# Attention inside a hybrid block: TensorE's order fixed by hand, transposes two key blocks ahead and in turn with products, low parts against the values' high part alone

## The chip, the cores and the metric

One Trainium2 chip, one core. The metric is the device time of one execution in microseconds (us), as a median of several runs.

## The reference, cut to what matters

The kernel computes a whole block of a streaming encoder: a norm, forgetting attention beside a state space model, gates, an output projection, a second norm and a convolutional feed-forward part. The change touches the attention alone:

```python
D_MODEL, SEQ, N_META = 1024, 1024, 16        # 16 meta tokens stand ahead: 1040 positions
ATTN_HEADS, ATTN_HEAD_DIM = 8, 64

def block(args):                             # one block of queries, all heads
    qb, fqb, qp = args
    s = jnp.einsum('bqhd,bkhd->bhqk', qb, k) * scale
    s = s + fq[..., None] - fk               # F[t] - F[s], cumulated log of the forget gate
    mask = k_pos[None, :] <= qp[:, None]
    s = jnp.where(mask[None, None], s, -1e30)
    p = jax.nn.softmax(s, axis=-1)
    return jnp.einsum('bhqk,bkhd->bqhd', p, v)
```

Everything is float32.

## The kernel before

**Float32 by halves.** TensorE is fed fp32r operands. A float32 number is split into a high and a low part, and a product becomes several matmuls. A projection takes three for each 128 of depth: high by high (L170), low by high (L171), high by low (L172).

**Tiles.** The queries are nine tiles: tile 0 has the 16 meta positions, tiles 1 to 8 have 128 each. A query tile c sees `KS[c] = 16 + 128 c` keys. The eight heads go in four pairs. While a pair is attended, TensorE also computes the next pair's queries and keys (`project_qk`, 16 matmuls of depth 128 by three for each part of 384, 384 or 272 columns) and some chunks of the gates (`gate_chunk`, 342 columns each, L499 reads them). These matmuls are called fill here. They write `mm`.

**Scores** (`scores`, for one query tile). Two matmuls (L825, L826) for each bank of at most 512 keys write `sp`, of which there are two PSUM buffers. Tile 7 has two banks (456, 456 keys), tile 8 has three (352, 352, 336). VectorE adds the forget row `fb` to a bank and takes the running least value (L831, into `pt` and `mx`); the diagonal 128 x 128 is a reduction of its own, against a masked copy `fm` from GpSimd (L814). So tile 7's second bank takes two reductions (328 and 128 wide), tile 8's third also two (208 and 128). Then ScalarE's exponential (L836), VectorE's reciprocal (L837), and GpSimd's multiplication (L838).

**Products** (`pv`, for one unit). A unit is one head and a pair of query tiles, (1,2), (3,4), (5,6) or (7,8), or the meta tile alone. The probabilities are transposed by TensorE, 128 x 128 each, into `tp` (two PSUM buffers); ScalarE copies that into the high part `th` (L872), VectorE makes the low part `tl` (L137). One group has two key blocks, up to four transposes, L868. The 16 meta keys have their own transposes (L854) and their own `tm` (one buffer, L855 on ScalarE, then L137 on VectorE). The values lie in `vt` as 128 columns for a head: 64 of their high part, 64 of their low part. Both `th` and `tl` are multiplied with all 128 columns (L891), `tm` likewise (L880), and sum up in one PSUM bank `po` (one buffer). At a unit's end ScalarE copies the lower half (L895) and VectorE adds the upper half (L896) into `ob`, which goes to DRAM.

**Order.** The program issues the scores of unit u+1 ahead of the products of unit u, and within a unit the transposes of the next group ahead of the products of this one. `fill()` releases a share of the fill at each group. It ties only the first matmul of a share, to the fifth last mark; beyond that a list scheduler with its own estimates of time decides where TensorE's instructions stand. PE, DVE, ACT, POOL and SP each work through their rows in order. The program text of one query tile's banks:

```python
for b in range(nb):
    ps = s_ps()                              # two PSUM buffers
    PE.matmul(ps, Qs, Ks, start=True, stop=False)
    PE.matmul(ps, qz, kl, start=False, stop=True)
    ...                                      # VectorE's reductions of this bank
```

Of the kernel before, what the change touches and what calls it, by code (L numbers as in the profile page):

```python
# [25 lines left out]
H = 8  # L26
# [32 lines left out]
def block_kernel(ctx, tc, x, meta, xbt, x0t, g1t, w_q, w_k, w_v, w_f, w_u, w_g, b_f, w_ao, lam_d, bw_d, cw_d,  # L59
# [25 lines left out]
    def po_ps():  # L85
        return pp.tile([P, 512], F, tag="po", name="po", bufs=1)
# [49 lines left out]
    def split_lo(eng, out_, src, hi):  # L136
        return eng.tensor_tensor(out_, src, hi.bitcast(F), ALU.subtract)  # L137
# [39 lines left out]
    def run(gen):  # L177
        for _ in gen:
            pass
# [612 lines left out]
    st_a = ExitStack()  # L792
    qps.append(pool(st_k, "qkB", side="left"))
    ap = pool(st_a, "attn", side="left")
    tm = ap.tile([P, 256], R, name="tm")
    GP.memset(tm.bitcast(F), 0.0)
    KS = [META + P * c for c in range(len(TILES))]
    qzero = [[ap.tile([P, P], R, name=f"qz{e}{j}") for j in range(2)] for e in range(2)]
    for e in range(2):
        for z in qzero[e]:  # L800
            GP.memset(z[64 - 64 * e:P - 64 * e].bitcast(F), 0.0)

    def scores(t_, e, c, fb):
        t, n = TILES[c]
# [11 lines left out]
        pt = ap.tile([P, L], F, tag="pt", name="pt", bufs=4)  # L816
        mx = ap.tile([P, 4], F, tag="mx", name="mx", bufs=4)
        low = 3e38
        nb = -(-kc // 512)
        w = -(-kc // nb // 8) * 8  # L820
# [1 line left out]
        for b in range(nb):  # L822
            a0, a1 = b * w, min(kc, b * w + w)
            ps = s_ps()
            PE.matmul(ps[:m_, :a1 - a0], Qs[:, t:t + m_], Ks[:, a0:a1], start=True, stop=False)  # L825
            PE.matmul(ps[:m_, :a1 - a0], qz[:, :m_], t_["kl"][:, a0:a1], start=False, stop=True)  # L826
            for lo, hi, src in ((a0, min(a1, dg), fb), (max(a0, dg), a1, None)):
                if hi <= lo:
                    continue
                s_ = fb[:n, lo:hi] if src is not None else fm[:n, lo - dg:hi - dg]  # L830
                V.tensor_tensor_reduce(out=pt[:n, lo:hi], in0=ps[:n, lo - a0:hi - a0], in1=s_, scale=-0.125,  # L831
                                       scalar=low, op0=ALU.add, op1=ALU.min, accum_out=mx[:n, ns:ns + 1])
                low = mx[:n, ns:ns + 1]
                ns += 1
        nm = ap.tile([P, 2], F, tag="nm", name="nm", bufs=4)
        S.activation(pt[:n, :kc], pt[:n, :kc], AF.Exp, bias=low, scale=-1.0, accum_out=nm[:n, 0:1])  # L836
        V.reciprocal(nm[:n, 1:2], nm[:n, 0:1])  # L837
        GP.tensor_scalar(pt[:n, :kc], pt[:n, :kc], nm[:n, 1:2], 1.0, ALU.mult, ALU.mult)  # L838
        return pt

    def pv(h, cs, pts, ob):
        e = h % 2
        t, n = TILES[cs[0]]
        w = n * len(cs)
        po = po_ps()
        groups = [(j, j + 1) for j in range(1, cs[-1], 2)]

        def order(grp):
            return grp[::-1] if grp[-1] > cs[0] else grp

        def meta_keys():
            tp = t_ps()
            for ci, p_ in enumerate(pts):
                PE.transpose(tp[:META, ci * n:ci * n + n], p_[:n, :META], ident[:n, :n])  # L854
            S.copy(tm[:META, :w], tp[:META, :w])  # L855
            split_lo(V, tm[32:32 + META, :w], tp[:META, :w], tm[:META, :w])

        def turn(grp):
            tp = t_ps()
            z = 0  # L860
            for gi, kk in enumerate(order(grp)):
                for ci, p_ in enumerate(pts):
                    k0 = TILES[kk][0]
                    o = (gi * len(pts) + ci) * n
                    if kk > cs[ci]:
                        z = o + n
                        continue
                    PE.transpose(tp[:, o:o + n], p_[:n, k0:k0 + P], ident)  # L868
            tw = len(grp) * w
            th = ap.tile([P, 512], R, tag="th", name="th", bufs=2)  # L870
            tl = ap.tile([P, 512], R, tag="tl", name="tl", bufs=2)
            S.copy(th[:, z:tw], tp[:, z:tw])  # L872
            split_lo(V, tl[:, z:tw], tp[:, z:tw], th[:, z:tw])
            return th, tl

        meta_keys()
        nxt = turn(groups[0]) if groups else None
        if groups:
            fill()
        marks.append(PE.matmul(po[:, :w], vt[:, 0, h, :], tm[:, :w], start=True, stop=not groups,  # L880
                               skip_group_check=True))
        for g_, grp in enumerate(groups):
            th, tl = nxt
            if g_ + 1 < len(groups):
                nxt = turn(groups[g_ + 1])
            fill()
            for gi, kk in enumerate(order(grp)):
                last = kk == order(groups[-1])[-1]
                q0 = n if kk > cs[0] else 0
                for t_ in (th, tl):  # L890
                    mk = PE.matmul(po[:, q0:w], vt[:, kk, h, :], t_[:, gi * w + q0:gi * w + w], start=False,  # L891
                                   stop=last and t_ is tl, skip_group_check=True)
            marks.append(mk)
        o_ = ob[64 * e:64 * e + 64, :w]
        S.copy(o_, po[64:, :w])  # L895
        V.tensor_tensor(o_, po[:64, :w], o_, ALU.add)  # L896

    GA = [2, 1, 1, 3]
    SLACK = 5
    QKN = 2 * len(BLK) * 3 * KD  # L900
    GAN = len(QBLK) * 3 * KD
    HOOKS = 2 * sum(1 + (c + 1) // 2 for c in range(1, len(TILES), 2))
    stream = iter(())
    left = [0, 0]
    marks = []

    def fill():
        k = -(-left[0] // max(1, left[1]))
        left[1] -= 1
        anchor = marks[-SLACK] if len(marks) >= SLACK else None  # L910
        for _ in range(k):
            if left[0] > 0:
                left[0] -= 1
                mm = next(stream, None)
                if mm is not None and anchor is not None:
                    tc.add_manual_dep(mm.ins, anchor.ins.name, mybir.DependencyInfo(
                        mybir.DependencyClass.NoSync, mybir.DependencyReason.DATA), reason="spread")
                    anchor = None

    def chain_(*gens):  # L920
        for g_ in gens:
# [16 lines left out]
    done = 0  # L938
    for pr in range(H // 2):
        fbs = []  # L940
        for e in range(2):
            fb = ap.tile([P, L], F, tag="fb", name="fb", bufs=2)
            SY.dma_start(fb, f_d[2 * pr + e].partition_broadcast(P))
            fbs.append(fb)
        gens, cnt = [], 0
        last_pair = pr == H // 2 - 1
        if not last_pair:
            qk_next = qk_tiles(pr + 1)
            gens.append(project_qk(pr + 1, qk_next))
            cnt += QKN  # L950
        for i in range(done, done + GA[pr]):
            gens.append(gate_chunk(i, ap, True))
            cnt += GAN
        done += GA[pr]
        stream = chain_(*gens)
        left[:] = [cnt, HOOKS]
        if pr == 0:
            for _ in range(24):
                next(stream)
                left[0] -= 1  # L960
        obs = {}

        def second(cs, e, pts):
            if e == 0:
                obs[cs] = ap.tile([P, 256], F, tag="ob", name="ob", bufs=1)
            pv(2 * pr + e, cs, pts, obs[cs])
            if e == 1:
                t, w = TILES[cs[0]][0], sum(TILES[c][1] for c in cs)
                if last_pair:
                    oh, ol = okeep[pr]  # L970
                    S.copy(oh[:, t:t + w], obs[cs][:, :w])
                    split_lo(V, ol[:, t:t + w], obs[cs][:, :w], oh[:, t:t + w])
                else:
                    SY.dma_start(o_d[P * pr:P * pr + P, t:t + w], obs[cs][:, :w])

        if last_pair:
            spare = qk_tiles(pr + 1)
            okeep[pr] = (spare["q0"], spare["q1"])
            okeep[0] = (spare["k0"], spare["k1"])
            of = spare["kl"].bitcast(F)  # L980
            SY.dma_start(of, o_d[:P])
            S.copy(spare["k0"], of)
            split_lo(GP, spare["k1"], of, spare["k0"])

        prev = None
        for n_unit, (cs, e) in enumerate(units):
            if 0 < pr < 3 and n_unit and n_unit % 2 == 0:
                out_weight_sums(4 * (pr - 1) + n_unit // 2 - 1, marks[-1])
            pts = [scores(qk, e, c, fbs[e]) for c in cs]
            if prev:  # L990
                second(*prev)
            prev = (cs, e, pts)
        second(*prev)
        run(stream)
        if pr < H // 2 - 1:
            qk = qk_next
    st_a.close()
    st_v.close()
    if "o_d" in dbg:
# [1050 lines left out]
```

## Time and profile before

| what | value |
|---|---|
| median of 3 runs | 1444.09 us (1443.51 to 1444.99) |
| profiled execution | 1441.98 us, span 1440.2 us |
| granted TensorE clock | 0.998 |
| instructions | 26318 |
| busy share of the span | PE 98%, PEld 93%, DVE 74%, ACT 50%, POOL 52% |
| attention stage | 339.27 to 619.73 us of the span |

The attention stage is counted here from the first fill matmul (L170) behind the values' projection (its last matmul, L130, starts at 339.04) to the first L170 behind the last L891. PE is TensorE's matmuls, PEld its weight loads, DVE VectorE, ACT ScalarE, POOL GpSimd, SP the queue that issues most DMAs. A row of the trace's timeline has a start in us, a duration in us, the engine, the line, the operation, output and inputs, and in brackets how long the engine was idle ahead of it and what released it. "x4" stands for four instructions that follow one another, with the time from the first's start to the last's end. Matmuls overlap: what counts for the pace is the time from one start to the next, not the duration of one.

### The profile page before, as it was taken

The numbers are of one execution on the slowest core, as the hardware profiler recorded it, in microseconds if no ns is written. First come the engines' busy times: TensorE is split into PE (matmuls) and PEld (weight loads), VectorE is DVE, ScalarE is ACT, GpSimd is POOL, SyncE is SP. The second block draws the span as 40 slices with busy tenths as digits, with TensorE's granted clock in tenths as the row PEclk, the third lists the DMA queues.
The fourth block names the chain that finished last, engine by engine and source line by source line (L and its number), as shares of the span: only waits on it lengthen the run. The fifth ranks groups of instructions, "written<-read, shape, count | busy, mean of one in ns | idle before, by whom it ended". The sixth has DMA issues, their size and how long they took to land.

```text
span 1440.2 us, 26318 instructions
## 1 busy us (share of the span) xinstructions
PE 1416.7 (98%) x9615; PEld 1337.7 (93%) x9615; DVE 1069.7 (74%) x2067; ACT 722.6 (50%) x1422; POOL 754.3 (52%) x824
## 2 busy tenths in 40 slices
PE   8999999999999999999999999999999999999997
PEld 8999999987999999999879999999999999887886
DVE  7999788843757676647469987888876876788767
ACT  7647585423646565533646443444444445643443
POOL 1642248632455546415861335555555545797795
PEclk9999999999999999999999999999999999999999
DMA  8776644531156322167964146667753327864443
GB/s 303 173 180 162 159 108 147 155 96 30 38 152 145 122 68 68 44 233 250 257 153 140 59 134 174 169 167 188 190 141 110 96 77 260 322 208 141 115 94 117
DMA packets 92966, 214.04 MB, mean 149 GB/s; under 512 B 15090, under 2 KB 22898, under 8 KB 92452
## 3 DMA queue, kind: packets, MB, share of 16 engines
q1 hardware_dynamic: 74132, 168.15, 35.5%
q0 software_dynamic: 17696, 41.29, 15.1%
q10 hardware_dynamic: 1008, 2.91, 0.6%
q8 instruction: 76, 1.25, 0.4%
q14 instruction: 54, 0.44, 0.1%
HBM read 170.88 MB, written 71.71 MB: 168 GB/s over the span
## 4 chain that ended last, share of the span: by engine, by line
PE 94%; DMA 2%; ACT 1%; DVE 1%; issue 1%; POOL 0%; SPq 0%; POOLq 0%; DVEq 0%; ACTq 0%
PE mm L172 5%; PE mm L170 5%; PE mm L171 5%; PE sp L233 4%; PE sp L232 4%; PE sp L234 4%; PE mm L232 3%; PE mm L234 3%; PE tp L232 3%; PE mm L233 3%; PE tp L233 3%; PE tp L234 3%; PE po L891 3%; PE tp L868 2%; PE mm L1573 2%; PE mm L1572 2%
## 5 line engine op out<-in xcount | busy, mean ns | idle before, releaser
L170 PE MATMUL mm<-xhi,whi 128*128 128x342 f32 (+2 forms) x480 | 157.7, 329 | 0.9 <-DVE q L137 0.9
L171 PE MATMUL mm<-xlo,whi 128*128 128x342 f32 (+2 forms) x480 | 155.9, 325 | 0.0
L172 PE MATMUL mm<-xhi,wlo 128*128 128x342 f32 (+2 forms) x480 | 155.7, 325 | 0.0
L1193 POOL TENSOR_TENSOR ov<-ov,og 128x1024 f32<-128x1024 f32 x21 | 50.8, 2421 | 119.4 <-ACT og L1192 117.1
L137 DVE TENSOR_TENSOR sw<-sf,sw 128x512 fp32r<-128x512 f32 x72 | 71.3, 990 | 45.9 <-ACT sw L1184 45.8
L1184 ACT CAST sw<-sf 128x512 fp32r<-128x512 f32 x72 | 44.9, 623 | 109.5 <-POOL sf L1331 69.9
L170 PEld LDWEIGHTS mm<-xhi,whi 128*128 128x128 f32 x480 | 90.4, 188 | 2.5 <-issue 1.7
L172 PEld LDWEIGHTS mm<-xhi,wlo 128*128 128x128 f32 x480 | 90.3, 188 | 0.6 <-issue 0.2
L171 PEld LDWEIGHTS mm<-xlo,whi 128*128 128x128 f32 x480 | 90.5, 189 | 0.3
L1331 POOL TENSOR_TENSOR sf<-raw,sf 128x512 f32<-128x512 f32 x36 | 61.7, 1714 | 39.2 <-DVE sw L137 39.1
L234 PE MATMUL mm<-xhi,sw 128*128 128x258 f32 (+1 forms) x288 | 81.0, 281 | 0.0
L232 PE MATMUL mm<-xhi,sw 128*128 128x258 f32 (+1 forms) x288 | 80.8, 280 | 0.0
L233 PE MATMUL mm<-xlo,sw 128*128 128x258 f32 (+1 forms) x288 | 80.7, 280 | 0.0
L1331 POOL TENSOR_TENSOR sf<-raw 128x512 f32<-128x512 f32 x36 | 48.8, 1355 | 60.8 <-DMA raw<-in_w_up_dram 35.6
L838 POOL TENSOR_SCALAR pt<-pt,nm 128x144 f32<-128x144 f32 (+4 forms) x72 | 52.2, 726 | 52.5 <-DVE nm L837 47.9
L836 ACT ACTIVATE pt<-pt,mx 128x144 f32<-128x144 f32 (+4 forms) x72 | 53.0, 736 | 36.0 <-DVE mx L831 35.3
L1383 DVE SCALAR_TENSOR_TENSOR ov<-hv,cwt,ov 128x1024 f32<-128x1024 f32 x36 | 69.2, 1921 | 0.4 <-ACT ov L1381 0.4
L1184 ACT CAST sw<-raw 128x512 fp32r<-128x512 f32 x70 | 43.0, 621 | 46.4 <-PE sp L234 24.2
L137 DVE TENSOR_TENSOR tl<-tp,th 128x512 fp32r<-128x512 f32 (+1 forms) x80 | 50.9, 636 | 14.6 <-ACT th L872 12.8
L137 DVE TENSOR_TENSOR sw<-raw,sw 128x512 fp32r<-128x512 f32 x70 | 56.8, 814 | 5.2 <-ACT sw L1184 5.0
L814 POOL TENSOR_SCALAR_AFFINE_SELECT fm<-fb 128x128 f32<-128x128 f32 (+1 forms) x72 | 20.8, 292 | 74.5 <-DMA fb<-f_d 38.1
L872 ACT CAST th<-tp 128x512 fp32r<-128x512 f32 (+1 forms) x80 | 43.4, 542 | 25.2 <-PE tp L868 22.1
(724 smaller groups left out, 5739.7 us busy)
## 6 DMA issues: line engine op xcount, KB each, us to landing
raw<-in_w_up_dram SPq DMA_DIRECT2D x44, 512.0 KB, 3.7
t_d<-in_w_dn_dram POOLq DMA_DIRECT2D x44, 256.0 KB, 7.0
wr<-t_d SPq DMA_DIRECT2D x44, 256.0 KB, 4.0
ar<-a_d SPq DMA_DIRECT2D x41, 256.0 KB, 5.4
a_d<-ov SPq DMA_DIRECT2D x18, 512.0 KB, 2.6
wr<-in_w_dn_dram SPq DMA_DIRECT2D x33, 256.0 KB, 3.8
t_d<-in_w_dn_dram SPq DMA_DIRECT2D x22, 256.0 KB, 4.3
t_d<-t_d SPq DMA_DIRECT2D x22, 256.0 KB, 5.1
```

Of the source, the lines that this page charges most:

```text
L137: return eng.tensor_tensor(out_, src, hi.bitcast(F), ALU.subtract)
L170: yield PE.matmul(ps, whi[:, i, :], ahi[:, i], start=(i == 0), stop=False)
L171: yield PE.matmul(ps, whi[:, i, :], alo[:, i], start=False, stop=False)
L172: yield PE.matmul(ps, wlo[:, i, :], ahi[:, i], start=False, stop=(i == k - 1))
L232: PE.matmul(ps, a[0][:, i], bh, start=(i == 0 and not joins), stop=False, skip_group_check=True)
L233: PE.matmul(ps, a[0][:, i], bl, start=False, stop=False, skip_group_check=True)
L234: PE.matmul(ps, a[1][:, i], bh, start=False, stop=(i == kh - 1), skip_group_check=True)
L836: S.activation(pt[:n, :kc], pt[:n, :kc], AF.Exp, bias=low, scale=-1.0, accum_out=nm[:n, 0:1])
L838: GP.tensor_scalar(pt[:n, :kc], pt[:n, :kc], nm[:n, 1:2], 1.0, ALU.mult, ALU.mult)
L1184: S.copy(hi, src)
L1331: sums.append(GP.tensor_tensor(f_, a, b, op))
L1383: V.scalar_tensor_tensor(out=o, in0=h_[:, j:SEQ + j], scalar=cwc(j, m), in1=o, op0=ALU.mult, op1=ALU.add)
```

## The change

- Each matmul and transpose of the attention, and each fill matmul in it, is tied to the one ahead of it (`pin`), so TensorE's order there is that of the program. The list scheduler still orders the other engines' instructions.
- The work of all pairs is one sequence of steps. A unit has one step for the meta keys and one for each group of two key blocks. In step k, the transposes of step k+2 are issued one by one in turn with the products of step k, and the copies into `th` and `tl` follow. Before, the transposes of a group stood one group ahead, as one block.
- Of a step's products the low parts come first. They multiply `vt`'s high 64 columns alone (L913, 64 x 256 out), then the high parts all 128 columns (L916).
- Scores are issued two units ahead instead of one (`ahead`): behind a unit's third last step the tiles but the last, behind its second last step the last tile.
- The meta query tile has no unit of its own. It stands with tiles 1 and 2 in one unit of 272 queries. Its eight 16-column products, evictions and adds, and four DMAs are gone; its `pt` lies in tile 1's buffer.
- Fill is issued at each step's end by a quota; units ending at tile 2, 4, 6, 8 have the weights 1.2, 1.0, 0.95, 0.9.

The lines move: L825/L826 become L836/L837, L831 L842, L836 L847, L838 L849, L854/L855 L868/L871, L868 L894, L872 L900, L880 L879, L891 L913 (low) and L916 (high), L895/L896 L925/L926.

```diff
-    tm = ap.tile([P, 256], R, name="tm")
+    tm = ap.tile([P, META + 256], R, name="tm")
+    def pin(inst):
+        if pinned[0] is not None:
+            after(inst, pinned[0])
+        pinned[0] = inst
+        return inst
...
-            PE.matmul(ps[:m_, :a1 - a0], Qs[:, t:t + m_], Ks[:, a0:a1], start=True, stop=False)
-            PE.matmul(ps[:m_, :a1 - a0], qz[:, :m_], t_["kl"][:, a0:a1], start=False, stop=True)
+            pin(PE.matmul(ps[:m_, :a1 - a0], Qs[:, t:t + m_], Ks[:, a0:a1], start=True, stop=False))
+            pin(PE.matmul(ps[:m_, :a1 - a0], qz[:, :m_], t_["kl"][:, a0:a1], start=False, stop=True))
...
+            def products():
+                th, tl = parts
+                low, high = [], []
+                for gi, kk in enumerate(order(grp)):
+                    q0 = P if kk > cs[0] else 0
+                    a, b = off + q0, slice(gi * 256 + q0, gi * 256 + 256)
+                    last = grp == groups[-1] and gi == 1
+                    low.append(lambda kk=kk, a=a, b=b: PE.matmul(
+                        bank[0][:DH, a:w], vt[:, kk, h, :DH], tl[:, b], start=False, stop=False,
+                        skip_group_check=True))
+                    high.append(lambda kk=kk, a=a, b=b, last=last: PE.matmul(
+                        bank[0][:, a:w], vt[:, kk, h, :], th[:, b], start=False, stop=last, skip_group_check=True))
+                return low + high
...
+    UW = {2: 1.2, 4: 1.0, 6: 0.95, 8: 0.9}
...
+    def fill(part):
+        quota[0] += quota[1] * part
+        n = int(quota[0])
+        quota[0] -= n
+        take(n)
...
-    units = [((0,), e) for e in range(2)] + [((c, c + 1), e) for c in range(1, len(TILES), 2) for e in range(2)]
+    shapes = [((0, 1, 2) if c == 1 else (c, c + 1), e) for c in range(1, len(TILES), 2) for e in range(2)]
+    units = [(pr, cs, e) for pr in range(NP) for cs, e in shapes]
...
+    stream, cnt = fill_of(0)
+    take(24)
+    cnt -= 24
+    for u, n in ((0, 14), (1, 14)):
+        scores_of(u, 0)
+        take(n // 2)
+        scores_of(u, 1)
+        take(n - n // 2)
+        cnt -= n
+    n_steps = [1 + cs[-1] // 2 for _, cs, _ in units]
+    ends = [sum(n_steps[:u + 1]) - 1 for u in range(len(units))]
...
+    def ahead(k):
+        for which in range(2):
+            if k + 2 - which in ends:
+                scores_of(ends.index(k + 2 - which) + 2, which)
...
+    for k in range(ends[-1] + 1):
...
+        todo, split = turns(k + 2)
+        mul = products()
+        if len(mul) > 1:
+            both = [mk for n in range(4) for mk in (todo[n:n + 1] + mul[n:n + 1])]
+        else:
+            both = todo + mul
+        for mk in both:
+            mk = pin(mk())
+        marks.append(mk)
+        if split:
+            split()
+        if evict:
+            evict()
+        ahead(k)
+        fill(1 / n_steps[u])
```

Where the rows stand, at the place where the scores of tile 8 are made, second pair, first head. PE before, from the first bank of tile 8 (`sp`, 352 wide) to the second; `mm` rows are fill, `tp` transposes, `po` products:

```order
L825 MATMUL sp<-k_4192,q_4190 128x352
L826 MATMUL sp<-kl,qz_4178 128x352
L891 MATMUL po<-tl,vt 128x128
L891 MATMUL po<-th,vt 128x256
L891 MATMUL po<-tl,vt 128x256
L868 MATMUL tp<-ident,pt 128x128 x4
L170 MATMUL mm<-xhi,whi 128x342
L171 MATMUL mm<-xlo,whi 128x342
L825 MATMUL sp<-k_4192,q_4190 128x352
L826 MATMUL sp<-kl,qz_4178 128x352
```

Sixteen rows of fill and four transposes then stand between the second bank and the third. PE now, from the second last step of tiles 5 and 6 (its transposes are those of the next unit's meta keys) to the third bank:

```order
L868 MATMUL tp<-ident,pt 16x128
L913 MATMUL po<-tl,vt 64x256
L868 MATMUL tp<-ident,pt 16x128
L913 MATMUL po<-tl,vt 64x256
L916 MATMUL po<-th,vt 128x256 x2
L836 MATMUL sp<-k_4188,q_4186 128x352
L837 MATMUL sp<-kl,qz_4178 128x352
L836 MATMUL sp<-k_4188,q_4186 128x352
L837 MATMUL sp<-kl,qz_4178 128x352
L836 MATMUL sp<-k_4188,q_4186 128x336
L837 MATMUL sp<-kl,qz_4178 128x336
```

The three banks now follow one another with nothing between them, seven fill rows behind tile 7's two banks. DVE before, at the same place, from tile 7's first reduction to tile 8's second (`kl` is the low part of the next pair's keys):

```order
L831 ISA pt,mx<-sp,fb 128x456
L831 ISA mx 128x1
L137 TENSOR_TENSOR tl<-tp,th 128x384
L831 ISA pt,mx<-sp,fb,mx 128x328
L831 ISA mx 128x1
L831 ISA pt,mx<-sp,fm,mx 128x128
L831 ISA mx 128x1
L837 RECIPROCAL nm<-nm 128x1
L137 TENSOR_TENSOR tm<-tp,tm 16x256
L831 ISA pt,mx<-sp,fb 128x352
L831 ISA mx 128x1
L831 ISA pt,mx<-sp,fb,mx 128x352
```

DVE now, the same stretch:

```order
L842 ISA pt,mx<-sp,fb 128x456
L842 ISA mx 128x1
L137 TENSOR_TENSOR kl<-mm,k_5331 64x384
L137 TENSOR_TENSOR kl<-mm,k_5332 64x384
L137 TENSOR_TENSOR tl<-tp,th 128x384
L842 ISA pt,mx<-sp,fb,mx 128x328
L842 ISA mx 128x1
L137 TENSOR_TENSOR tm<-tp,tm 16x256
L842 ISA pt,mx<-sp,fb 128x352
L842 ISA mx 128x1
L842 ISA pt,mx<-sp,fm,mx 128x128
L842 ISA mx 128x1
```

Two `kl` rows now stand between tile 7's first and second reduction (before, they came behind tile 8's second), and the 128 wide reduction that ends tile 7's second bank stands behind tile 8's first.

More of the change, by code (lines that the diff above doesn't have):

```diff
@@ L834, in scores @@
                 ns += 1
-        nm = ap.tile([P, 2], F, tag="nm", name="nm", bufs=4)
+        nm = mx[:, 4:]
         S.activation(pt[:n, :kc], pt[:n, :kc], AF.Exp, bias=low, scale=-1.0, accum_out=nm[:n, 0:1])
@@ L852, in meta_keys @@
             tp = t_ps()
[L853 to L893, printed above, removed]
@@ L894, in pv, with one, split @@
-        o_ = ob[64 * e:64 * e + 64, :w]
-        S.copy(o_, po[64:, :w])
-        V.tensor_tensor(o_, po[:64, :w], o_, ALU.add)
+            def one(p_, o, n):
+                return lambda: PE.transpose(tp[:META, o:o + n], p_[:n, :META], ident[:n, :n])
+            def split():
+                S.copy(tm[:META, :w], tp[:META, :w])
+                split_lo(V, tm[32:32 + META, :w], tp[:META, :w], tm[:META, :w])
+            head = [one(pts[0], 0, META)] if off else []
+            return head + [one(p_, off + P * ci, P) for ci, p_ in enumerate(main)], split
@@ L898, in block_kernel, with take @@
+        return [(u, t_, p_, evict if k == len(groups) else None)
+                for k, (t_, p_) in enumerate([(meta_turns, meta_products)] + [of(g_) for g_ in groups])]
     GA = [2, 1, 1, 3]
-    SLACK = 5
+    UW = {2: 1.2, 4: 1.0, 6: 0.95, 8: 0.9}
     QKN = 2 * len(BLK) * 3 * KD
     GAN = len(QBLK) * 3 * KD
-    HOOKS = 2 * sum(1 + (c + 1) // 2 for c in range(1, len(TILES), 2))
     stream = iter(())
-    left = [0, 0]
+    quota = [0.0, 0.0]
     marks = []
[L907 to L918, printed above, removed]
+    def take(n):
+        for _ in range(n):
+            mm = next(stream, None)
+            if mm is not None:
+                pin(mm)
@@ L951, in block_kernel @@
[L951 to L963, printed above, removed]
-            if e == 0:
[L965 to L992, printed above, removed]
@@ new lines, in block_kernel, with turns @@
+    n_steps = [1 + cs[-1] // 2 for _, cs, _ in units]
+    ends = [sum(n_steps[:u + 1]) - 1 for u in range(len(units))]
+    steps = {}
+    def turns(k):
+        if k > ends[-1]:
+            return [], None
+        if k not in steps:
+            u = next(u for u, last in enumerate(ends) if k <= last)
+            for n, st in enumerate(steps_of(u)):
+                steps[ends[u] - n_steps[u] + 1 + n] = st
+        return steps[k][1]()
+    def ahead(k):
+        for which in range(2):
+            if k + 2 - which in ends:
+                scores_of(ends.index(k + 2 - which) + 2, which)
@@ L997, in block_kernel @@
+    for mm in stream:
+        pin(mm)
     st_a.close()
```

128 lines of the change are left out of this document (105 added, 23 removed).

## The prediction

> **What bounds the kernel now.** I read the page's busy shares and chain first, then a table by stage, then the groups of the attention stage on PE, then what PE waits for there, then its timeline.
>
> ```profile
> PE 1416.7 (98%) x9615; PEld 1337.7 (93%) x9615; DVE 1069.7 (74%) x2067; ACT 722.6 (50%) x1422; POOL 754.3 (52%) x824
> PE 94%; DMA 2%; ACT 1%; DVE 1%; issue 1%; POOL 0%; SPq 0%; POOLq 0%; DVEq 0%; ACTq 0%
> ```
>
> The chain is TensorE's. The change does nothing outside the attention, so only that stage counts. In the table the columns behind the length are the busy times of PE, PEld, DVE, ACT and POOL:
>
> ```profile
> 339.27:362.00 22.73, 20.03 (x127) 18.59 (x126) 12.74 (x54) 11.49 (x32) 10.97 (x28) 1.00 0.19 52
> 614.90:619.73 4.83, 4.13 (x30) 3.43 (x28) 3.04 (x5) 2.52 (x5) 1.13 (x1) 1.00 0.49 157
> 339.27:619.73 280.46, 273.14 (x1895) 262.89 (x1894) 181.10 (x644) 160.57 (x388) 143.13 (x248) 1.00 0.32 88
> ```
>
> PE is idle for 7.3 us of 280.46 by this table, but matmuls overlap and their ends are modelled, so I price them by the distance between starts. In these rows a 342-column matmul takes 0.16 us (0.157 over longer rows of them), four transposes 0.36 together with the change to a product (0.109 each), a 256-column product 0.12:
>
> ```profile
> 560.68 0.32 PE L170 MATMUL mm<-xhi,whi 128*128 128x342 f32 x1
> 560.84 0.32 PE L171 MATMUL mm<-xlo,whi 128*128 128x342 f32 x1
> ...
> 614.90 0.60 PE L868 MATMUL tp<-ident,pt 128*128 128x128 f32 x4
> 615.26 0.36 PE L880 MATMUL po<-tm,vt 128*128 128x256 f32 x1
> 615.46 0.28 PE L891 MATMUL po<-th,vt 128*128 128x256 f32 x1
> 615.58 0.28 PE L891 MATMUL po<-tl,vt 128*128 128x256 f32 x1
> ```
>
> The counts (L171 and L172 have those of L170, `tl` those of `th`):
>
> ```profile
> L170 PE MATMUL mm<-xhi,whi 128*128 128x342 f32 x168 | 56.0, 334 | 0.0
> L868 PE MATMUL tp<-ident,pt 128*128 128x128 f32 x288 | 45.5, 272 | 0.0
> L891 PE MATMUL po<-th,vt 128*128 128x256 f32 x128 | 38.0, 303 | 0.0
> L170 PE MATMUL mm<-xhi,whi 128*128 128x384 f32 x96 | 33.3, 346 | 0.9 <-DVE q L137 0.9
> L170 PE MATMUL mm<-xhi,whi 128*128 128x272 f32 x48 | 14.1, 293 | 0.0
> L891 PE MATMUL po<-th,vt 128*128 128x128 f32 x32 | 7.3, 228 | 0.1
> ```
>
> Fill: 504 x 0.157 + 288 x 0.176 + 144 x 0.125 = 147.8 us (384 and 272 columns in proportion). Transposes of the keys 288 x 0.109 = 31.4, of the meta keys 64 x 0.109 = 7.0 and eight small ones 2.4. Products 256 x 0.118 + 64 x 0.059 = 34.0, meta products 40 of them 4.7. Scores: 76,032 columns, counted in the program, at 0.457 ns (0.157 us over 342) 34.8. One thing on top: a diagonal group, two 128-wide products ahead of two 256-wide ones, lasts 0.47 from the first of these rows to the second, where its columns are worth 0.354; 32 x 0.11 = 3.6, of which 3.3 taken, since some are hidden.
>
> ```profile
> 564.76 0.22 PE L891 MATMUL po<-th,vt 128*128 128x128 f32 x1
> ...
> 565.23 0.49 PE L868 MATMUL tp<-ident,pt 128*128 128x128 f32 x3
> ```
>
> In all 265.4 us of work, so 15.1 us of the stage are waits and lost distance. By the timeline 5.5 of them lie ahead of 362, about 2.2 behind 614.90 (the last unit has no fill left to stand between `tl` and its product), and 7.4 between. Who is waited for:
>
> ```profile
> PE sp L825 <- DVE mx L831: 1.8, 4, 0.7
> PE po L880 <- DVE tm L137: 1.7, 3, 0.8
> PE po L880 <- DVE ob L896: 1.0, 1, 1.0
> PE po L891 <- DVE tl L137: 0.9, 3, 0.3
> PE mm L170 <- DVE q L137: 0.9, 1, 0.9
> ...
> 358.10 0.39 PE L825 MATMUL sp<-k,q 128*128 128x264 f32 x1 [0.66 <-DVE mx L831]
> ...
> 521.22 0.39 PE L880 MATMUL po<-tm,vt 128*128 128x256 f32 x1 [0.75 <-DVE tm L137]
> ```
>
> The row at 358.10 is a score matmul that needs a third bank while VectorE still reads the first: that is what score banks cost when they follow one another directly.
>
> **The change, part by part.** *Work.* The exposed 0.11 at a diagonal group goes where a transpose stands between the narrow products: taken at 2.5 of the 3.3 us, bounds 0 and 3.3. The eight 16-column meta products go, 0.9 (from 8 x 0.11). The low products have 64 columns of weights and the same 256 moving columns: 0, since their pace is set by what moves. Transposes in turn with products: 0 too. Whether a transpose is bound by its weight load can be seen here, two transposes with 16 columns of weights:
>
> ```profile
> 564.01 0.38 PE L854 MATMUL tp<-ident,pt 128*16 128x128 f32 x2
> ```
>
> 0.38 less one duration of 0.272 is 0.108 for the second, the same as with 128 columns of weights (0.60 less 0.272 over three: 0.109). The load is not the limit. The Trainium skill ("TensorE: Matmul & The Clock Gate", section LDWEIGHTS (loading the stationary operand)) gives a weight load about columns/1.2 ns, 107 ns for 128 columns, which is nearly the transposes' distance and would make it load-bound; the 16-column row disagrees, and what the rule would give if it held is rival three. Work in sum: -3.4.
>
> *Waits that go.* Products now use `th` and `tl` made two steps before, so L891's waits for `tl` go; the end of the stage keeps fill between its steps: -2.2. At the start the meta query tile's wait for `ob` (1.0) and the banks back to back (most of the 1.8) go; the first keys' wait for `q` (0.9) and the first softmax stay: 5.5 becomes 2.4, estimated. The 7.4 in the middle are of the kinds listed above, and are counted anew below.
>
> *Waits that come.* Everything on TensorE is queued behind a score matmul that waits for its bank, since the order is fixed: before, the scheduler had put a dozen matmuls between tile 8's banks. So I follow VectorE through the unit of tiles 5 and 6, in pairs two and three where a block of the next keys is evicted there. Durations:
>
> ```profile
> L831 DVE CUSTOM_DVE_ANT_0 pt<-sp,fb 128x456 f32<-128x456 f32 x8 | 5.0, 630 | 1.0 <-PE tp L868 0.5
> L137 DVE TENSOR_TENSOR kl<-mm,k 64x384 fp32r<-64x384 f32 x12 | 6.7, 555 | 2.8 <-ACT k L610 2.7
> L137 DVE TENSOR_TENSOR tl<-tp,th 128x384 fp32r<-128x384 f32 x32 | 17.8, 555 | 2.3 <-ACT th L872 1.9
> L831 DVE CUSTOM_DVE_ANT_0 pt<-sp,fb,mx 128x328 f32<-128x328 f32 x8 | 4.5, 557 | 2.8 <-PE sp L826 2.8
> L137 DVE TENSOR_TENSOR tm<-tp,tm 16x256 fp32r<-16x256 f32 x32 | 13.2, 414 | 6.9 <-ACT tm L855 5.6
> L831 DVE CUSTOM_DVE_ANT_0 pt<-sp,fb 128x352 f32<-128x352 f32 x8 | 4.2, 525 | 3.4 <-PE sp L826 3.4
> L831 DVE CUSTOM_DVE_ANT_0 pt<-sp,fm,mx 128x128 f32<-128x128 f32 x64 | 22.2, 349 | 5.0 <-DVE mx L831 0.5
> L837 DVE RECIPROCAL nm<-nm 128x1 f32<-128x1 f32 x64 | 10.4, 163 | 23.3 <-ACT pt L836 22.0 <-ACT tm L855 0.7
> ```
>
> Let 0 be the start of the step's transposes and products. Three transposes and four products take 0.80, tile 7's two banks (456 and 456 columns, two matmuls each) 0.83, to 1.63; seven fill matmuls of 0.176 to 2.86; two transposes and four products to 3.55; tile 8's first bank 0.32, to about 3.87. Its second bank goes where tile 7's second was, which is free when VectorE has finished the 328 and the 128 reduction. VectorE: 456 from 1.25 to 2.0 with its reading, two `kl` 1.1, `tl` 0.56, 328 0.56, `tm` 0.41, 352 0.53, 128 0.35, with the readings' few hundredths about 5.4 (bounds 5.2 and 5.7). TensorE stands for 1.5 us. Tile 8's other banks are made by 6.0, and its least value is known at about 7.2 (352, 208, a reciprocal and 128 behind 5.4 and one another). Its exponential, the `th` and the `ob` copy stand on ScalarE ahead of the add that frees `po`; with a reading of 0.2 behind the exponential, they end at about 9.9:
>
> ```profile
> L836 ACT ACTIVATE pt<-pt,mx 128x1040 f32<-128x1040 f32 x8 | 9.3, 1168 | 4.7 <-DVE mx L831 4.7
> L872 ACT CAST th<-tp 128x512 fp32r<-128x512 f32 x48 | 28.0, 584 | 15.8 <-PE tp L868 14.3 <-DVE tl L137 0.7
> L895 ACT COPY ob<-po 64x256 f32<-64x256 f32 x31 | 11.5, 369 | 15.7 <-PE po L891 14.4 <-DMA o_d<-ob 0.7
> L896 DVE TENSOR_TENSOR ob<-po,ob 64x256 f32<-64x256 f32 x31 | 12.9, 417 | 7.1 <-ACT ob L895 6.5
> ```
>
> TensorE, already late, wants `po` for the next meta product (L879) at about 9.4 (6.0, two shares of fill of 1.1 each, one group of 0.8 and four transposes): another 0.5 to 0.7. So 2.2 in each of four units: 8.8. In pairs one and four no `kl` stands there: the same sums give 0.75 at two and 1.1 at two, 3.7. At tiles 3 and 4 (tile 6 has two banks behind tile 5's two) 0.75 in three units with a block of keys and 1.0 over the rest: 3.2. From the first head's last unit to the second's 4 x 0.55, at the change of pairs 3 x 0.65: 4.2. Small units and other pieces 1.5. With the start's 2.4 the waits after are 23.8. The lower bound has each bank wait at half and the start at 2: 17. The upper bound has the `kl` units at 3.5 and the others at 1.5 apiece: 36.
>
> Other moves cost nothing on the path: GpSimd's POOL rows (143 of 280 us busy) and SP's DMAs gain no work, four small output DMAs go; the forget rows are loaded as early as before relative to their first reader, whose cover at the start is the 24 fill matmuls.
>
> **Sum.** -3.4 work, -15.1 waits that were, +23.8 waits that will be: +5.3. The profiled execution's 1441.98 becomes 1447.3; it lies 2.1 below the median of the runs, 1444.09, which becomes 1449.4.
>
> **The rivals.** *Other side: VectorE and ScalarE keep up.* If the list scheduler's order on VectorE is kinder in time than my chain (the `kl` rows wait for ScalarE's key copies, and those end earlier because `mm` is evicted sooner), tile 7's second reduction is done when TensorE arrives; waits after fall to about 9 (start 2.4, and some 0.2 at each of 32 units), and the time is 1444.1 - 15.1 + 9 - 3.4 = 1434.6. The sign turns at 18.5 us of waits. For it: VectorE is busy 181 of 280 us; against it: the row at 358.10, and three banks for two buffers in a fixed order.
>
> *No difference.* Bank waits at half and the old ones gone: waits after 16 to 21, 1441.6 to 1446.6.
>
> *Weight loads set the transposes' pace.* Then a transpose between products hides its load: 218 of the 288 transposes stand beside a product and save 0.05 each, 10.9 us: 1438.5 with my waits. Against it stands the 16-column row.
>
> *Banks worse.* All waits at the upper bound: 36 - 15.1 - 3.4 is +17.5, 1461.6.
>
> **How the numbers follow.** About 0.2% (2.9 us) is what a measurement of this kernel can tell from no change. My forecast has 0.33, banks worse 0.12, no difference 0.22, VectorE keeps up 0.25, weight loads 0.08. Slower is then 0.45, same 0.22, faster 0.33. The range goes from 1433, just below the rival of the other side, to 1462, the upper bound; my forecast's own range is 1447 to 1455.
>
> **What would show it.** Right: the stage from the first L170 to the last product about 285.8 us long; PE idle ahead of L836, released by L842, in the units of tiles 5 and 6, above 1 us at places with `kl`; L879 waiting for `ob`; no wait of L913 or L916 for `tl`; the part up to 362 some 3 us shorter; distances of 0.109 at transposes with products between. Wrong: a stage below 278 us with L836's waits under 5 us in all (the rival of the other side), or transposes and products in turn at less than their sum of 0.227 (weight loads).

## The result: slower by 1.3%, and the profile after

The changed kernel takes 1461.53 us (1459.8 to 1462.9, 4 runs) against 1443.8 for the kernel before in the same comparison. The ratio is 1.0129 with a 95% interval of 1.0115 to 1.0143, which is 17 to 21 us. The profiled execution has a span of 1459.0 us at a granted clock of 0.999.

The page's busy shares and its chain, after:

```profile
PE 1417.7 (97%) x9607; PEld 1333.1 (91%) x9607; DVE 1074.8 (74%) x2050; ACT 722.7 (50%) x1405; POOL 756.0 (52%) x824
...
PE 88%; DVE 6%; ACT 2%; issue 2%; DMA 1%; POOL 0%; POOLq 0%; DVEq 0%; SPq 0%; ACTq 0%
```

The busy times hardly differ from before, and the chain does: 6% of the span now lies on VectorE (1% before) and 2% on ScalarE (1%). The table by stage, with the same columns as before; the stage again runs from the first L170 behind the values' projection to the first fill matmul behind the last product (an L171 here, 0.31 us ahead of the next L170):

```profile
633.00:638.08 5.08, 5.08 (x41) 5.01 (x41) 1.52 (x3) 1.07 (x2) 0.00 (x0) 1.00 0.00 0
340.38:638.08 297.70, 272.57 (x1885) 256.53 (x1884) 178.19 (x626) 159.17 (x369) 142.16 (x247) 1.00 0.29 81
```

The attention stage went from 280.46 to 297.70 us, 17.2 of the 18.8 us by which the spans differ. The end runs on without idle time, 5.08 of 5.08, where before it had 4.13 of 4.83. So the loss lies earlier. All of PE's waits in this stage, from the view of waits:

```profile
PE po L879 <- DVE ob L926: 14.2, 21, 1.1
PE sp L836 <- DVE mx L842: 9.1, 11, 1.4
PE tp L868 <- DVE tm L137: 1.6, 1, 1.6
```

Three kinds are left. The largest is the meta product, the first user of the one bank `po` in a unit: it waits for the add that empties the bank. Before, this was 1.0 us, once.

One such place after, the last unit, where no exponential is in the way; the timeline over all engines, rows of one place:

```profile
630.33 0.36 PE L916 MATMUL po<-th,vt 128*128 128x256 f32 x1
...
630.61 0.59 ACT L900 CAST th<-tp 128x512 fp32r<-128x512 f32 x1 [1.49 <-PE tp L894]
...
631.22 0.37 ACT L925 COPY ob<-po 64x256 f32<-64x256 f32 x1
631.23 0.69 DVE L137 TENSOR_TENSOR tl<-tp,th 128x512 fp32r<-128x512 f32 x1 [1.67 <-ACT th L900]
631.31 0.60 PE L894 MATMUL tp<-ident,pt 128*128 128x128 f32 x4
...
631.83 0.41 DVE L926 TENSOR_TENSOR ob<-po,ob 64x256 f32<-64x256 f32 x1
...
632.29 0.38 PE L879 MATMUL po<-tm,vt 128*128 128x256 f32 x1 [0.38 <-DVE ob L926]
```

And the same unit's place before:

```profile
613.25 0.28 PE L891 MATMUL po<-tl,vt 128*128 128x256 f32 x1
613.36 0.60 PE L868 MATMUL tp<-ident,pt 128*128 128x128 f32 x4
613.60 0.37 ACT L895 COPY ob<-po 64x256 f32<-64x256 f32 x1
...
614.00 0.59 ACT L872 CAST th<-tp 128x512 fp32r<-128x512 f32 x1
614.05 0.42 DVE L896 TENSOR_TENSOR ob<-po,ob 64x256 f32<-64x256 f32 x1
...
614.62 0.69 DVE L137 TENSOR_TENSOR tl<-tp,th 128x512 fp32r<-128x512 f32 x1
```

Read the order on ACT and on DVE. Before, the copy `ob` came ahead of `th` and the add ahead of `tl`: `po` was free 1.22 us after the last product began (613.25 to 614.47). After, `th` (0.59) stands ahead of the copy and `tl` (0.69) ahead of the add, and the bank is free after 1.91 us (630.33 to 632.24). TensorE had five fill matmuls and four transposes in between, to 631.67, and stood.

The place that the prediction worked through, in the second pair, on VectorE and PE:

```profile
533.74 0.63 DVE L842 CUSTOM_DVE_ANT_0 pt<-sp,fb 128x456 f32<-128x456 f32 x1 [2.02 <-PE sp L837]
...
534.29 1.12 DVE L137 TENSOR_TENSOR kl<-mm,k 64x384 fp32r<-64x384 f32 x2
...
535.45 0.56 DVE L137 TENSOR_TENSOR tl<-tp,th 128x384 fp32r<-128x384 f32 x1
...
535.92 0.55 DVE L842 CUSTOM_DVE_ANT_0 pt<-sp,fb,mx 128x328 f32<-128x328 f32 x1
536.04 0.32 PE L837 MATMUL sp<-kl,qz 128*128 128x352 f32 x1
...
537.40 0.34 DVE L842 CUSTOM_DVE_ANT_0 pt<-sp,fm,mx 128x128 f32<-128x128 f32 x1
537.54 0.43 PE L836 MATMUL sp<-k,q 128*128 128x352 f32 x1 [1.18 <-DVE mx L842]
```

With 0 at 532.33, the second bank came at 5.21; the prediction had 5.4. The same place's next meta product started at 542.72, and the add that frees `po` for it ended at 542.66, 10.3 on this scale; the prediction had 9.9.

To add up what such places cost, the tables below count lost distance: the time from one matmul's start to the next, less what its columns are worth at the prices of the prediction, where more than 0.2 us is over. It is put down to the matmul that came late. (Of four transposes ahead of a product, 0.08 us shows one matmul later: in the prediction's rows the product starts 0.36 us behind the first transpose, less than 4 x 0.109, and its own distance is 0.20 instead of 0.12. The count allows for that.)

| kernel | stage | ahead of meta products | ahead of scores | ahead of transposes |
|---|---|---|---|---|
| before | 280.46 us | 3.99 (6 places) | 2.59 (4) | 1.20 (3) |
| after | 297.70 us | 20.06 (23) | 10.84 (11) | 1.78 (1) |

Before, products lost 2.57 and fill 1.10 besides; after, neither lost anything. What lies below 0.2 us a place fell from 10.65 to 7.54; that includes the diagonal groups and the small matmuls that the prediction's sum counts as work.

### The profile page after: what moved, and what is told of

It is laid out like the page before. It is cut to its first block, busy times and chain, and to the rows that moved or that the text cites. A ratio compares the mean times of both kernels' runs of the same rounds, so it can differ in the third digit from the quotient of the medians.

```text
span 1459.0 us, 26230 instructions
## 1 busy us (share of the span) xinstructions
PE 1417.7 (97%) x9607; PEld 1333.1 (91%) x9607; DVE 1074.8 (74%) x2050; ACT 722.7 (50%) x1405; POOL 756.0 (52%) x824
## 4 chain that ended last, share of the span: by engine, by line
PE 88%; DVE 6%; ACT 2%; issue 2%; DMA 1%; POOL 0%; POOLq 0%; DVEq 0%; SPq 0%; ACTq 0%
PE sp L232 4%; PE sp L233 4%; PE sp L234 4%; PE mm L170 4%; PE mm L171 4%; PE mm L172 4%; PE tp L232 3%; PE tp L233 3%; PE tp L234 3%; PE mm L234 3%; PE mm L232 3%; PE mm L233 3%; DVE pt L842 2%; PE mm L1659 2%; PE mm L1657 2%
## 5 line engine op out<-in xcount | busy, mean ns | idle before, releaser
L170 PE MATMUL mm<-xhi,whi 128*128 128x342 f32 (+2 forms) x480 | 154.5, 322 | 0.1
L171 PE MATMUL mm<-xlo,whi 128*128 128x342 f32 (+2 forms) x480 | 154.0, 321 | 0.0
L170 PEld LDWEIGHTS mm<-xhi,whi 128*128 128x128 f32 x480 | 90.4, 188 | 1.0 <-issue 0.4
L171 PEld LDWEIGHTS mm<-xlo,whi 128*128 128x128 f32 x480 | 90.4, 188 | 0.1
L847 ACT ACTIVATE pt<-pt,mx 128x400 f32<-128x400 f32 (+5 forms) x72 | 53.0, 735 | 49.9 <-DVE mx L842 49.5
L820 POOL CAST qz<-q 64x128 fp32r<-64x128 f32 (+1 forms) x72 | 20.0, 281 | 97.0 <-PE sp L837 95.6
L849 POOL TENSOR_SCALAR pt<-pt,mx 128x400 f32<-128x400 f32 (+5 forms) x72 | 50.8, 706 | 34.7 <-DVE mx L848 34.4
L137 DVE TENSOR_TENSOR sw<-raw,sw 128x512 fp32r<-128x512 f32 x70 | 59.8, 857 | 3.6 <-ACT sw L1270 3.3
L900 ACT CAST th<-tp 128x512 fp32r<-128x512 f32 (+1 forms) x80 | 43.1, 539 | 37.4 <-PE po L916 18.0
```

Source lines behind the costliest of these rows:

```text
L170: yield PE.matmul(ps, whi[:, i, :], ahi[:, i], start=(i == 0), stop=False)
L171: yield PE.matmul(ps, whi[:, i, :], alo[:, i], start=False, stop=False)
```

## The experiments

Ratios are to the kernel before, run on the same chip. Its median was 1441.1 to 1442.7 us there, against 1443.8 in the result, so the ratios are to be compared and not the times in us.

### The eviction ahead of `th` and `tl`

```diff
-        if split:
-            split()
-        if evict:
-            evict()
+        firsts_ = evict() if evict else ()
+        seconds_ = split() if split else ()
+        for x_, y_ in zip(firsts_, seconds_):
+            after(y_, x_)                    # th behind the copy, tl behind the add
```

(The closures return their two instructions.)

> The changed kernel, with each unit's eviction (the ScalarE copy of po and VectorE's add) ordered ahead of the th and tl of the same step. Theory A (the one bank po comes free late, because th and tl stand ahead of the eviction in the two queues): the waits of the meta product L879 for ob, 14.2 us of idle and 20.1 us of lost distance, fall to about 4, those behind tile 8's exponential; time 1461.5 - 16 = 1445. Theory B (the time is lost to the score banks and to transposes in turn with products; the meta product's wait only shows time that would be lost a little later): within 3 us of 1461.5.

Ratio 1.0033 (1.0017 to 1.0048); 1445.18 us. The stage is 283.05 us, 14.7 shorter than after; the lost distance ahead of meta products fell from 20.06 to 3.84, while scores kept theirs (10.51). PE's waits:

```profile
PE sp L836 <- DVE mx L842: 8.7, 11, 1.4
PE po L879 <- DVE ob L925: 1.8, 7, 0.3
```

The last unit's place again, the one shown for the kernels before and after:

```profile
615.87 0.36 PE L915 MATMUL po<-th,vt 128*128 128x256 f32 x1
...
616.27 0.37 ACT L924 COPY ob<-po 64x256 f32<-64x256 f32 x1 [1.61 <-PE po L915]
...
616.66 0.59 ACT L901 CAST th<-tp 128x512 fp32r<-128x512 f32 x1
616.67 0.42 DVE L925 TENSOR_TENSOR ob<-po,ob 64x256 f32<-64x256 f32 x1 [1.57 <-ACT ob L924]
```

The bank is free 1.22 us after the last product began (615.87 to 617.09), as in the kernel before. Theory A holds, theory B does not: of the 16.2 us, 1.6 turned up again in smaller pieces elsewhere. By the ratios the kernel is 13.9 us shorter than after, where 16 were expected. The 3.84 that are left lie at eight places, each with an exponential ahead of the copy.

### Fill between the banks of tile 8

```diff
         for b in range(nb):
+            if gap and b == 1:               # tile 8 only: the step's whole fill
+                gap()
             ps = s_ps()
```

> The changed kernel, with the fill of the step that scores tile 8 moved between that tile's first and second bank (before, behind the third). Theory A2 (a score matmul stands for its bank while VectorE works off tile 7's second bank): 1.1 of about 1.4 us at four places and 0.6 at four go, 6 to 7 us, 1455; the waits of L838 for L844 fall from 9.1 us to about 3. Rival (VectorE is behind anyway, and the wait moves to the meta product's ob): those waits rise by as much, and the time stays at 1461.5 within 2.

Ratio 1.0051 (1.0033 to 1.0069); 1449.48 us. The stage is 287.76 us, 9.9 shorter than after. PE's waits:

```profile
PE po L881 <- DVE ob L928: 9.1, 20, 1.1
PE sp L838 <- DVE mx L844: 3.0, 5, 1.0
```

The lost distance at scores fell by 6.4 (10.84 to 4.46), as expected, and that ahead of meta products by 5.0 as well (20.06 to 15.04), which neither theory had. The trace shows why, at the same place of the second pair (last product at 534.04):

```profile
532.90 1.06 ACT L849 ACTIVATE pt<-pt,mx 128x912 f32<-128x912 f32 x1 [1.71 <-DVE mx L844]
...
534.37 0.59 ACT L902 CAST th<-tp 128x512 fp32r<-128x512 f32 x1 [0.32 <-PE tp L896]
...
534.98 0.37 ACT L927 COPY ob<-po 64x256 f32<-64x256 f32 x1
...
535.26 1.16 ACT L849 ACTIVATE pt<-pt,mx 128x1040 f32<-128x1040 f32 x1
```

At this place tile 8's exponential (1040 wide) now stands behind the eviction. In the changed kernel it stood ahead of `th` there, from 539.89 to 541.05, and pushed the copy to 541.64, 1.3 us behind the end of the last product. At the eight places of this kind the lost distance fell by 5.4 us, so the whole of the 5.0 lies there. In this trace one stretch of 3.4 us, from 354.5, ran at a granted clock of 0.50, which by estimate adds at most 1.7 us (half of it) to the stage.

### Both

> Both edits in the changed kernel: the eviction ordered ahead of th and tl, and the fill of tile 8's step between that tile's first and second bank. Theory (two separate waits, which the runs so far priced at 16.2 us for po and 6.4 us for the banks, of a stage of 297.7 us): the stage is 297.7 - 16.2 - 6.4 = 275.1 us, less a little more where the late banks pushed the eviction; against 280.5 before, the time is 0.3 to 0.5% below the kernel before. Rival (one wait gives way to the other, VectorE being the bound): no shorter than the eviction alone, 0.3% above the kernel before.

Ratio 0.9950 (0.9937 to 0.9962); 1435.78 us: faster than both kernels, by 5 to 9 us against the one before. The stage is 274.32 us, where 275.1 were expected; lost distance 2.78 ahead of meta products, 4.37 at scores and 2.07 at transposes. Its chain is TensorE's again, and PE's waits are:

```profile
PE 95%; DVE 2%; DMA 1%; ACT 1%; issue 1%; POOLq 0%; POOL 0%; DVEq 0%; SPq 0%; ACTq 0%
```

```profile
PE sp L838 <- DVE mx L844: 3.1, 6, 1.0
PE po L881 <- DVE ob L927: 2.0, 3, 1.5
PE tp L870 <- DVE tm L137: 1.6, 1, 1.6
```

1.73 of the 2.78 us come from one place and another cause. The copy waits there for the output DMA that reads the same `ob` tile, which has one buffer:

```profile
478.54 0.37 ACT L926 COPY ob<-po 64x256 f32<-64x256 f32 x1 [1.72 <-DMA o_d<-ob]
...
479.42 0.38 PE L881 MATMUL po<-tm,vt 128*128 128x256 f32 x1 [1.48 <-DVE ob L927]
```

### Low parts against all 128 columns, and 64 columns in the kernel before

In the changed kernel, back to 128 columns:

```diff
-    bank[0][:DH, a:w], vt[:, kk, h, :DH], tl[:, b], ...
+    bank[0][:, a:w], vt[:, kk, h, :], tl[:, b], ...
```

> The changed kernel, with the low parts multiplied by all 128 columns of the values as before. My reading of weight loads (a product's pace is set by the columns that move): the same as the changed kernel, 1461.5 within 2. Rival (the weight load sets the pace, so 64 columns save half a load of 0.05 us in each of 160 products): 1461.5 + 8 = 1469.

Ratio 1.0127 (1.0111 to 1.0143), the changed kernel's own 1.0129. And the kernel before with 64 columns for `tl` in L891:

> The kernel before, with one part of the change alone: the low parts multiply the values' high 64 columns, all else as before. Both readings of the runs so far (the 128-column version of the changed kernel was no slower): within 0.2% of the kernel before.

Ratio 1.0004 (0.9992 to 1.0015). The narrower low products change nothing in either kernel.

### Transposes as a block instead of in turn

```diff
-            both = [mk for n in range(4) for mk in (todo[n:n + 1] + mul[n:n + 1])]
+            both = todo + mul
```

> The changed kernel, with each step's transposes as one block ahead of its products instead of in turn with them. If turns cost and save nothing: 1461.5 within 2, with the exposed 0.11 us of a diagonal group back (up to +3). If a product hides a transpose's weight load: 218 x 0.05 = 11 us longer, 1472. If turns cost time (each change between the two kinds loses something): shorter by more than 3, below 1458.

Ratio 1.0101 (1.0084 to 1.0119), 4 us shorter than after by the ratios, which by my lines speaks for turns that cost time. The stage is 3.3 us shorter, and the lost distance ahead of meta products 3.4 (20.06 to 16.64). That left two readings: turns cost time, or the block lets `th` start earlier and the eviction behind it. So the block once more, with the eviction ahead:

> The changed kernel with the eviction ordered ahead of th and tl, and each step's transposes as a block ahead of its products. The block alone was 4 us shorter than the changed kernel, and its lost distance at the meta product fell by 3.4 us. If that was only th starting earlier and so the eviction behind it (turns themselves cost nothing): with the eviction already ahead, the same as with the eviction alone, 1.0033 of the kernel before within 0.15%. If turns cost TensorE time: 3 to 4 us shorter again, 1.001 or below.

Ratio 1.0028 (1.0015 to 1.0041), against 1.0033 with turns; the stage is 285.01 us against 283.05. Of these 2.0 us up to 1.7, by estimate, are one stretch of 3.4 us, from 355.6, at a granted clock of 0.50. Within the 0.13% (2 us) of the interval turns cost nothing and save nothing; the 4 us came through the eviction.

### Fill ahead of the meta product

```diff
-        for mk in both:
+        first = len(mul) == 1
+        for mk in (todo if first else both):
             mk = pin(mk())
+        if first:
+            fill(1 / n_steps[u])             # and none behind this step
+            mk = pin(mul[0]())
```

> The changed kernel, with the eviction where it is, but the fill of a unit's first step issued ahead of its meta product instead of behind it, which puts 5 to 17 matmuls, 0.9 to 2.7 us, between the last product of a unit and the next use of po. Theory A (the eviction is late by 0.6 to 1.4 us a unit): nearly all of the 20 us of lost distance at L879 goes, as with the eviction ahead: 1461.5 - 16 = 1445, if the later steps don't wait for th and tl in turn. Theory B (VectorE and ScalarE are the bound, the wait moves to the next product): the waits for tl or for banks rise by as much, above 1456.

Ratio 1.0126 (1.0112 to 1.0140): no gain. My expectation missed. The lost distance ahead of meta products went from 20.06 to 1.57, as theory A has it, and that at scores rose from 10.84 (11 places) to 22.98 (20). PE's waits:

```profile
PE sp L836 <- DVE mx L842: 19.8, 20, 2.0
...
PE po L879 <- DVE ob L926: 1.1, 3, 0.4
```

The fill that stood behind a unit's first step had parted the scores of tiles 5 and 6 in the units of three steps: eight of the twenty places are now between tile 6's two 392-wide banks, 0.9 to 2.1 us each. In this fixed order the same fill covers only one of the two.

The scores took 12.1 of the 18.5 us that left the meta products. Part of the rest is the clock: in three stretches of this stage, from 455.4, 520.3 and 530.5, the granted clock (the number after POOL's busy time) was half.

```profile
455.40:458.81 3.41, 3.41 (x15) 3.31 (x13) 1.16 (x6) 1.79 (x4) 2.33 (x5) 0.50 0.00 0
520.30:523.71 3.41, 3.41 (x19) 3.41 (x17) 1.12 (x6) 1.86 (x4) 2.18 (x5) 0.50 0.56 154
530.50:533.91 3.41, 3.41 (x11) 3.32 (x12) 1.16 (x8) 1.97 (x4) 1.91 (x5) 0.50 0.02 5
```

Half of 3 x 3.41 is 5.1 us, by estimate the most that they cost; without them the time would be 1456 or more, still far from 1445. All four runs of this kernel had a mean clock of 0.994 or 0.995, those of the changed kernel 0.998 or 0.999. That the longer waits bring the clock down is not shown.

### TensorE's order left to the scheduler

```diff
     def pin(inst):
-        if pinned[0] is not None:
-            after(inst, pinned[0])
-        pinned[0] = inst
         return inst
```

> The changed kernel without the ties between TensorE's matmuls: the program order of the steps is the same, and the list scheduler may move matmuls past each other. Theory (it is the fixed order that makes each late bank a stop of everything behind it): the lost distance at score and meta products falls from 31 us to under 15, time about 1445. Rival (the scheduler, which does not see the late eviction, keeps nearly the program's order): above 1455.

Ratio 1.0041 (1.0026 to 1.0057), 1449.27 us, between the two lines and nearer to the first. The stage is 288.62 us. Lost distance fell to 0.67 ahead of meta products and 4.40 at scores, and a new one came: 14.52 us at 20 transposes. PE's largest wait:

```profile
PE tp L891 <- DVE tl L137: 6.4, 10, 0.9
```

The scheduler put fill where the fixed order waits, and moved transposes to where their PSUM bank is still being read for `tl`. Its 19.6 us for the three kinds compare with 32.7 of the fixed order and 9.2 of the fixed order with both edits above. Of the 17.2 us by which the fixed order's stage is longer than before, 9.1 went.

## Why the prediction was right or wrong

**Direction and place: right, the size a third.** It had a slower kernel by 5.3 us, and 17.7 came. It had the loss in the attention stage, behind score banks and the `po` bank, with TensorE's other work queued behind the waiting matmul. Removing the two waits turned the sign, at about the price that the lost distances gave.

**Work, -3.4: right.** The distances around products, over what their columns are worth and counted at places below 0.2 us, fell from 4.2 to 1.4 us in all, 2.8 for the 2.5 that the diagonal groups were to give; the 0.9 of the eight 16-column products was not measured by itself. Nothing was gained by 64 columns (1.0127, 1.0004), nothing by turns (1.0028 against 1.0033). The pairs of a transpose and a product keep the sum of their distances, 0.22 to 0.23 us, as in these rows after:

```profile
633.15 0.27 PE L894 MATMUL tp<-ident,pt 128*128 128x128 f32 x1
633.18 0.36 PE L913 MATMUL po<-tl,vt 128*64 128x256 f32 x1
633.38 0.27 PE L894 MATMUL tp<-ident,pt 128*128 128x128 f32 x1
633.40 0.36 PE L913 MATMUL po<-tl,vt 128*64 128x256 f32 x1
633.60 0.27 PE L894 MATMUL tp<-ident,pt 128*128 128x128 f32 x1
```

So the rival of weight loads falls, though the loads did get shorter. The weight loads of the low products, from the groups of the changed kernel and of its 128-column version:

```profile
L913 PEld LDWEIGHTS po<-tl,vt 128*64 128x64 f32 x160 | 21.8, 136 | 3.2
```

```profile
L913 PEld LDWEIGHTS po<-tl,vt 128*128 128x128 f32 x160 | 30.4, 194 | 2.8
```

58 ns less for 64 columns less. The Trainium skill ("TensorE: Matmul & The Clock Gate", section LDWEIGHTS (loading the stationary operand)) gives columns/1.2 ns for a load. By an estimate from that rule, 64 columns are 53 ns: the traces come near it in the difference (58), and not in the whole (136 and 194 ns busy). But the load lies beside the matmul ahead, and nothing on the path became shorter.

**Waits that go: right but for the start.** No product waits for `tl`, and the end of the stage has no idle time. The start hardly got shorter. Counted in the same way, over 0.2 us at a time and ahead of 362, it lost 3.8 us before and 3.5 after (4.9 and 4.7 with the small pieces), where the prediction had 5.5 become 2.4. Two bank waits stayed (0.6 and 1.2), and a transpose lost 1.8 for `tm`'s reading of its bank.

**Banks: a little too high.** The prediction had 6.0 at the four places with `kl`, 3.7 less some `po` at the others, and 3.2 at tile 6: up to 12.9. Measured behind the start: 5.8, 2.4 and 0.9, together 9.1. (VectorE's durations in the prediction's chain add up to 5.5 and not 5.4. Of the upper bound of 36, 22.1 follow from terms that it names, and the other 13.9 are some nine places at 1.5 that it does not name.)

**`po`: the step that failed.** "Another 0.5 to 0.7" in the units of tiles 5 and 6, and 4.2 at the changes of head and pair, is about 7 us. Measured: 20.06 at 23 of 32 units. The failed step is the chain that frees the one bank `po`: the prediction priced it in part where tile 8's scores are made and at the changes, and had no term for it behind the units of tiles 3 and 4.

| places | predicted | measured |
|---|---|---|
| units of tiles 5 and 6, with `kl` (4) | 2.0 to 2.8 | 5.0 |
| units of tiles 5 and 6, pairs one and four (4) | a part of 3.7 | 4.1 |
| changes of head and pair (7) | 4.2 | 5.0 |
| behind the units of tiles 3 and 4 (8) | no term | 6.0 |

At the place worked through above it was followed step by step, with `th` ahead of the copy, but without `tl` ahead of the add. There tile 8's least value was known at 7.5 (the exponential starts at 539.89), 0.3 later than said; and the copy ended at 542.01, `tl` stood ahead, and the add began at 542.26. The loss was 1.15, for 0.5 to 0.7. ScalarE's and VectorE's rows after have `th` directly ahead of the copy and `tl` ahead of the add at all 31 changes of unit, as the program text has `split()` ahead of `evict()`. Where nothing else is in the way that is 0.7 us more (1.91 against 1.22 in the rows above), and the fill and transposes between the last product and the meta product are too short for it. At 19 of the 23 places an exponential ending behind the last product delayed `th`, too. With the eviction ahead of `th` and `tl` alone, and the exponentials where they stood, 16.2 of the 20.1 us went.

**The upper rival's time, 1461.6, was met, but by luck:** it had the banks at their bounds, and they were below my middle value.

**The sum against the trace.** 5.3 predicted, 13.1 more at `po`, 1.1 more at the start, 3.8 less at the banks: 15.7. The 1.5 that are left to 17.2 are put down to pieces under 0.2 us, if the work is as predicted: the stage less the 262.0 us of work has 35.7 us of waits, 32.7 of them in the table; the prediction gave 1.5 to the 3.0 of small pieces.

What remains open: whether the eviction could also be ordered ahead of the exponential, which stands in front of it at the eight places that lost 3.84 us with the eviction ahead of `th` and `tl`. It was not tried.

## What to carry to other kernels

When an accumulator has one bank and TensorE sets the pace, try its eviction ahead of what else is ready at the same moment on the evicting engines: a cast of 0.6 us and a subtraction of 0.7 us ahead of it, at 31 changes of unit, cost 14 us here. A fixed order of TensorE can turn a late release into a stop of everything behind it (9.1 of 17.2 us went when the ties did), so the distance between a bank's last use and its next has to be counted in matmuls, for every buffer, at the commonest place first. Fill is spent once: moved ahead of one wait, it uncovers another (20.1 to 1.6 at `po`, 10.8 to 23.0 at the score banks).

## What the runs showed of the hardware

In the changed kernel a transpose and a 256-column product in turn take 0.22 to 0.24 us together; in blocks their distances are 0.109 and 0.118, which add up to 0.227; and with 128 columns of weights for the low products the median of a pair is 0.23. The granted clock fell to 0.50 for stretches of 3.41 us: three in the trace with fill ahead of the meta product, one each in three others, and none in the attention stage of the kernels before and after. What brings it down is not shown. Unexpected was how a wait spreads over engines: shortening the score banks' wait by 6.4 us took another 5.0 off the `po` bank, because tile 8's exponential then left ScalarE free at the eviction.
